# A hybrid decoder layer: the MLP's down projection by Strassen's seven products, token-major

## The chip, the cores and the metric

One core of a Trainium2 chip runs the whole layer in one launch. A core has five engines that work side by side and wait for each other through semaphores: TensorE (PE: matrix products into PSUM), VectorE (DVE), ScalarE (ACT), GpSimd (POOL) and SyncE (SP, which here only issues DMAs). Transfers run on 16 DMA engines that all queues share. The metric is the device time of one execution in microseconds, the median of the runs; lower is better.

## The reference

A pre-norm decoder layer on 512 tokens of width 1024, in float32. The first half (a gated DeltaNet, a convolution module and a cross-attention, merged through gates) is not touched. The second half is the conv-gated MLP, and a final norm:

```
h = rmsnorm(x, norm_ffn)
up = h @ w_up                                             # 1024 -> 2 x 2816
g_f = causal_dwconv(up[..., :2816], ffn_dw_w) + ffn_dw_b  # three taps along the tokens
x = x + (silu(g_f) * up[..., 2816:]) @ w_down             # 2816 -> 1024
return rmsnorm(x, norm_final)
```

## The kernel before

**Layout and precision.** Activations lie channel-major: a tile is 128 channels (partitions) by 512 tokens. Every large product is computed from high and low parts: `split` (L142) has ScalarE cast a tile to the matmul format (the high part) and VectorE subtract (the low part), and `proj` (L253) issues three matmuls for each slice of 128 of the contraction: high x high, high x low, low x high. The weight tile is the stationary operand, the activations move, 512 columns at a time.

**Weights.** They lie in DRAM as chunks of eight 128x128 tiles in order of use (512 KB). `fetch` (L223) loads chunk by chunk on SP's queue into four buffers `raw`, and splits each into `whi` and `wlo`, four buffers each. `wtile` (L244) asks for four chunks ahead. A tile is used by three matmuls, so a chunk lasts for 24.

**Order.** TensorE's and SP's instructions stand in the order in which the code issues them; for the other engines a scheduler chooses an order from its own estimates when the program is built. `run` (L153) interleaves a main generator with side generators, one step for each slice of `proj`. `paced` ties an instruction behind the last matmul issued, and `behind` (L104) ties VectorE's.

**The MLP.** `proj_o` (L1012) ends the first half and leaves the residual in eight tiles `x1`, and the scaled input's high and low parts `fh`, `fl`. `fnorm` (L1037) makes the norm's factors `rfb`. `ffn_up` (L1049) takes 22 slices j of the 2816 hidden channels; for each it makes the gate's product (tile `mm`) and the values' (tile `g`), 24 matmuls each; VectorE multiplies by `rfb` (L1059), ScalarE and VectorE do the taps (L1061, L1063), ScalarE the SiLU (L135), POOL multiplies by `rfb` again (L1067), VectorE by the values (L1069), and the result is split into `ah[j]`, `al[j]`, kept in SBUF.

`ffn_down` (L1084) takes output tiles of 128 channels: 22 slices, 66 matmuls into one PSUM bank; VectorE adds the result to `x1` (L1088), ScalarE squares it (L1090), VectorE sums the squares (L1094), ScalarE multiplies by the final norm's gain (L1096). That is so for seven tiles. The eighth is done in two halves of 256 tokens (`last_tile`, L1133), so that the norm and the stores of one half stand beside the other's matmuls. `final_norm` (L1109) sums the squares over channels with matmuls by a vector (L1114), takes the power -1/2 on POOL (L1116), spreads the factors over partitions with two transposes (L292), multiplies (L1127, L1125) and stores through ACT's and SP's queues (L1128).

Of the kernel before, what the change touches and what calls it, by code (L numbers as in the profile page):

```python
# [15 lines left out]
P = 128  # L16
# [6 lines left out]
WARM = 10  # L23
NSLOT = 74
# [13 lines left out]
        ("lnw", 4), ("lnb", 4), ("gateb", 24), ("nffn", KD), ("fdw", NJ * 3), ("fdb", NJ), ("nfin", KD),  # L38
# [16 lines left out]
def hybrid_kernel(ctx: ExitStack, tc: tile.TileContext, xT, memT, xtok, mtok, wall, vecs, cms, yT):  # L55
# [166 lines left out]

    def fetch(upto):  # L223
        while state[0] < min(upto, wall.shape[0]):
# [822 lines left out]
    ah, al = [], []  # L1047

    def ffn_up():  # L1049
        for j in range(NJ):  # L1050
            ps = MM()
            yield from proj(ps, fh, fl)
            pv = G()
            gv = proj(pv, fh, fl)
            for _ in range(8 if j == 0 else 1):
                next(gv)
                yield
            g = T(n="fg")
            V.tensor_tensor(g, ps, rfb, op=ALU.mult)  # L1059
# [10 lines left out]
            if j == NJ - 1:  # L1070
                free(*fh, *fl)
            a, b = T(dt=F32R, n="ah"), T(dt=F32R, n="al")
            split(c, a, b)
            free(c)
            ah.append(a)
            al.append(b)

    gf = fnorm()
    run(ffn_up(), (gf, 1))

    nsq = [None, None]
    HS = S // 2

    def ffn_down():  # L1084
        for o in range(KD - 1):
            ps = MM()
            yield from proj(ps, ah, al)
            V.tensor_tensor(x1[o], x1[o], ps, op=ALU.add)  # L1088
            s = T(n="sq")
            A.activation(s, x1[o], AF.Square)  # L1090
            if o == 0:
                nsq[0] = s
            else:
                V.tensor_tensor(nsq[0], nsq[0], s, op=ALU.add)  # L1094
                free(s)
            A.activation(x1[o], x1[o], AF.Copy, scale=vc("nfin", o))  # L1096

    rn, r0 = C((P, NT)), C((P, NT))

    def other_tiles():  # L1100

        yield from pause(6)
        ps = SM((P, NT))
        for t in range(NT):
            PE.matmul(ps[:, t:t + 1], nsq[0][:, sl(t)], mean, start=True, stop=True)
        V.tensor_scalar(r0, ps, EPS, None, op0=ALU.add)
        yield

    def final_norm(t0, t1):  # L1109

        c, n = slice(t0 * P, t1 * P), t1 - t0
        ps = SM((P, NT))
        for t in range(t0, t1):
            PE.matmul(ps[:, t:t + 1], nsq[1][:, sl(t)], mean, start=True, stop=True)  # L1114
        V.tensor_tensor(rn[:, t0:t1], r0[:, t0:t1], ps[:, t0:t1], op=ALU.add)
        G_.tensor_tensor(rn[:, t0:t1], rn[:, t0:t1], mhalf[:, :n], op=ALU.pow)  # L1116
        yield from pause(4)
        ps = G((P, n * P))
        bcast(ps, rn[:, t0:t1], n)
        w = 4 // n  # L1120
        for o in range(0, KD, w):
            y = T((P, w, n * P), n="y")
            for k in range(w):
                if o + k == KD - 1:
                    V.scalar_tensor_tensor(y[:, k], x1[o + k][:, c], vc("nfin", o + k), ps, op0=ALU.mult, op1=ALU.mult)  # L1125
                else:
                    V.tensor_tensor(y[:, k], x1[o + k][:, c], ps, op=ALU.mult)  # L1127
            (nc.sync if o // w % 2 else A).dma_start(yT[o:o + w, :, c].rearrange("o p c -> p o c"), y)  # L1128
        yield

    nsq[1] = T(n="sq")

    def last_tile(t0, t1):  # L1133
        c, n = slice(t0 * P, t1 * P), (t1 - t0) * P
        ps = MM()
        yield from proj(ps[:, :n], [t[:, c] for t in ah], [t[:, c] for t in al], at=pos[0])
        V.tensor_tensor(x1[KD - 1][:, c], x1[KD - 1][:, c], ps[:, :n], op=ALU.add)
        A.activation(nsq[1][:, c], x1[KD - 1][:, c], AF.Square)

    run(ffn_down())  # L1140
    run(last_tile(0, 2), (other_tiles(), 1))
    run(last_tile(2, 4), (chain(pause(4), final_norm(0, 2)), 1))
    drain(final_norm(2, 4))


# [11 lines left out]
def _layout(i):  # L1157
# [26 lines left out]
    parts.append(_tiles(g["w_down"][0]))  # L1184
# [7 lines left out]
    def taps(c):  # L1192
# [7 lines left out]
           "fdb": _cols(g["ffn_dw_b"][0]), "nfin": _cols(g["norm_final"]),  # L1200
# [17 lines left out]
    return {"xT": xT, "memT": memT, "xtok": g["x"][0].reshape(NT, P, D), "mtok": g["mem"][0].reshape(2, P, D), "wall": wall, "vecs": vecs, "cms": cms}  # L1218


_INS = ["xT", "memT", "xtok", "mtok", "wall", "vecs", "cms"]
# [19 lines left out]
```

## Time and profile before

| | us |
|---|---|
| median of 3 runs (lowest, highest) | 867.12 (866.92, 867.3) |
| the profiled execution | 866.9 |
| its span, first to last instruction | 865.1 |
| TensorE / VectorE / ScalarE / POOL busy | 853.5 / 541.8 / 356.5 / 92.7 |

Busy times are to be read against the span. A matmul's own duration is longer than its step: matmuls overlap in the array, so what one costs is the distance between two starts. The up projection goes from 493 to 733 us, the down projection from 733.4 to 855.5, and the end follows. An instruction that starts later than its predecessor's end has waited; the timeline shows in brackets for how long and for whom.

### The profile page before, as it was taken

The page shows a single profiled execution, that of the slowest core. Times are in us where ns is not written, and L with a number is a line of the kernel's source. Part 1 is how long each engine was busy: PE and PEld are TensorE (multiplying, and loading weights), DVE is VectorE, ACT ScalarE, POOL GpSimd, SP SyncE. Part 2 cuts the span into 40 slices and gives each one's busy share as a digit, 9 for nine tenths or more (in the row PEclk, how much of TensorE's full clock was granted, in tenths as well). Part 3 has the DMA queues.
Part 4 walks back from the last instruction along what each step waited for, and adds up shares of the span by engine and source line. Part 5 has one row for each costly group of instructions (what it writes and reads, how often), then busy time and mean ns, then how long its engine had stood idle before and what let it go on. Part 6 is the DMA issues. An engine that isn't in the chain of part 4 may idle for free.

```text
span 865.1 us, 11006 instructions
## 1 busy us (share of the span) xinstructions
PE 853.5 (99%) x4260; PEld 707.7 (82%) x4260; DVE 541.8 (63%) x852; ACT 356.5 (41%) x613; POOL 92.7 (11%) x103
## 2 busy tenths in 40 slices
PE   9999999999999999999999999999999999999996
PEld 7888788688877888888888888888888888888885
DVE  5885799869989999582385565555555555223223
ACT  7854676443333445353334443333333333223220
POOL 0100003400043010150000011111111111000000
PEclk9999999999999999999999999999999999999998
DMA  9753121352071222222334223332232322233202
GB/s 314 290 183 124 66 74 49 97 127 93 1 220 49 73 74 73 98 96 98 106 130 147 95 84 98 98 97 98 98 98 97 98 98 98 97 98 98 73 1 97
DMA packets 43556, 90.97 MB, mean 105 GB/s; under 512 B 15728, under 2 KB 20080, under 8 KB 43504
## 3 DMA queue, kind: packets, MB, share of 16 engines
q1 hardware_dynamic: 36144, 87.65, 30.5%
q10 hardware_dynamic: 7360, 2.62, 1.2%
q8 instruction: 33, 0.54, 0.3%
q14 instruction: 19, 0.16, 0.1%
HBM read 86.59 MB, written 3.67 MB: 104 GB/s over the span
## 4 chain that ended last, share of the span: by engine, by line
PE 93%; DVE 4%; issue 2%; ACT 1%; DMA 0%; POOL 0%; POOLq 0%; SPq 0%; DVEq 0%; ACTq 0%
PE mm L260 23%; PE mm L262 22%; PE mm L261 22%; PE g L262 5%; PE g L260 5%; PE g L261 5%; DVE wlo L146 1%; PE g L561 1%; PE g L559 1%; PE g L560 1%; DVE qkv L626 0%; DVE cc L597 0%; PE mm L397 0%; PE mm L396 0%; PE mm L398 0%
## 5 line engine op out<-in xcount | busy, mean ns | idle before, releaser
L145 ACT CAST whi<-raw 128x1024 fp32r<-128x1024 f32 (+1 forms) x150 | 154.4, 1029 | 300.5 <-PE mm L261 228.3
L146 DVE TENSOR_TENSOR wlo<-raw,whi 128x1024 fp32r<-128x1024 f32 (+1 forms) x150 | 181.1, 1207 | 112.9 <-ACT whi L145 112.0
L260 PE MATMUL mm<-hh,whi 128*128 128x512 f32 x352 | 143.4, 407 | 0.0
L262 PE MATMUL mm<-hh,wlo 128*128 128x512 f32 x352 | 137.6, 391 | 0.0
L261 PE MATMUL mm<-hl,whi 128*128 128x512 f32 x352 | 137.3, 390 | 0.0
L597 DVE SCALAR_TENSOR_TENSOR cc<-u,vec,cc 128x507 f32<-128x507 f32 (+19 forms) x120 | 87.1, 732 | 1.0
L262 PEld LDWEIGHTS mm<-hh,wlo 128*128 128x128 f32 x352 | 66.1, 188 | 14.5
L260 PEld LDWEIGHTS mm<-hh,whi 128*128 128x128 f32 x352 | 66.2, 188 | 13.3 <-issue 1.5
L261 PEld LDWEIGHTS mm<-hl,whi 128*128 128x128 f32 x352 | 66.3, 188 | 11.2
L260 PE MATMUL mm<-ah,whi 128*128 128x512 f32 (+1 forms) x198 | 72.6, 367 | 0.0
L261 PE MATMUL mm<-al,whi 128*128 128x512 f32 (+1 forms) x198 | 72.3, 365 | 0.0
L262 PE MATMUL mm<-ah,wlo 128*128 128x512 f32 (+1 forms) x198 | 72.3, 365 | 0.0
L260 PE MATMUL g<-fh,whi 128*128 128x512 f32 x176 | 68.6, 390 | 0.0
L260 PE MATMUL mm<-fh,whi 128*128 128x512 f32 x176 | 68.6, 390 | 0.0
L262 PE MATMUL g<-fh,wlo 128*128 128x512 f32 x176 | 68.5, 389 | 0.0
L262 PE MATMUL mm<-fh,wlo 128*128 128x512 f32 x176 | 68.5, 389 | 0.0
L261 PE MATMUL g<-fl,whi 128*128 128x512 f32 x176 | 68.5, 389 | 0.0
L261 PE MATMUL mm<-fl,whi 128*128 128x512 f32 x176 | 68.5, 389 | 0.0
L1067 POOL TENSOR_TENSOR fc<-fc,rfb 128x512 f32<-128x512 f32 x22 | 28.5, 1294 | 205.5 <-ACT fc L135 205.5
L1059 DVE TENSOR_TENSOR fg<-mm,rfb 128x512 f32<-128x512 f32 x22 | 15.2, 691 | 54.6 <-PE mm L262 54.6
L1069 DVE TENSOR_TENSOR fc<-fc,g 128x512 f32<-128x512 f32 x22 | 15.1, 688 | 46.9 <-POOL fc L1067 46.9
L261 PEld LDWEIGHTS mm<-al,whi 128*128 128x128 f32 x198 | 37.3, 189 | 6.1
(294 smaller groups left out, 1484.1 us busy)
## 6 DMA issues: line engine op xcount, KB each, us to landing
raw<-wall SPq DMA_DIRECT2D x142, 512.0 KB, 3.3
x<-xT SPq DMA_DIRECT2D x16, 256.0 KB, 4.2
raw<-wall SPq DMA_DIRECT2D x8, 256.0 KB, 5.8
tok<-xtok SPq DMA_DIRECT2D x8, 256.0 KB, 4.9
mraw<-memT SPq DMA_DIRECT2D x4, 256.0 KB, 6.2
tok<-mtok SPq DMA_DIRECT2D x4, 256.0 KB, 6.6
d_in<-at ACTq DMA_DIRECT2D x4, 256.0 KB, 3.0
yT<-y ACTq DMA_DIRECT2D x4, 256.0 KB, 2.4
```

The lines of the kernel that those rows point to most:

```text
L145: A.copy(hi, src)
L146: eng.tensor_tensor(lo, src, f(hi), op=ALU.subtract)
L260: PE.matmul(ps, hi, xh[k], start=(k == 0), stop=False)
L261: PE.matmul(ps, hi, xl[k], start=False, stop=False)
L262: last[0] = PE.matmul(ps, lo, xh[k], start=False, stop=(k == n - 1))
L559: PE.matmul(ps[h], hi, xh[k], start=(k == 0), stop=False)
L560: PE.matmul(ps[h], hi, xl[k], start=False, stop=False)
L561: PE.matmul(ps[h], lo, xh[k], start=False, stop=(k == KD - 1))
L597: paced(V.scalar_tensor_tensor(a[:, s:], u[c][:, :S - s], vc("dww", c * 31 + 30 - s), a[:, s:], op0=ALU.mult, op1=ALU.add))
L1059: V.tensor_tensor(g, ps, rfb, op=ALU.mult)
L1067: G_.tensor_tensor(c, c, rfb, op=ALU.mult)
L1069: V.tensor_tensor(c, c, pv, op=ALU.mult)
```

## The change

**Seven products.** The hidden channels are paired: the even slices of 128 are one half of the contraction, the odd ones the other. With 2 x 2 blocks (256 tokens; half the hidden channels; 512 output channels) the product is Strassen's, in Winograd's form, with seven block products in place of eight. The activations' slices are now the stationary operand (128 hidden channels by 128 tokens) and the weights move (512 output channels), so the result lies token-major: two PSUM banks of 128 tokens by 512 channels for each product. Each product is 11 slices x 2 token blocks x 3 matmuls.

**Sums of weights.** Four of the seven products need sums of weight blocks. `weight_sums` makes them in DRAM while the up projection runs: for each of 11 slices a plain DMA on SP's queue copies one summand (256 KB) to a DRAM tile, and three slots later a DMA on POOL's queue adds the second summand to it in place. A slot is 2 x SUMS = 6 steps, four sums take 4 x 14 slots. `blockfetch` then loads blocks, two at a time, in place of `fetch`.

**Sums of activations.** `ends` forms the differences of a pair of slices on VectorE, for the first EARLY = 8 pairs while the up projection runs; the other splits are issued from `prepare` during the down projection. POOL's product (L1067 before) goes to VectorE.

**Residual and norm.** `token_major` turns the residual by 32 transposes on TensorE, four at a time into the one bank `SM`, copied out by ScalarE. The products' results are added to it on VectorE (`upd`). The final norm's squares are now summed along the free dimension by ScalarE (`square`), and `store` scales and stores a block of 128 tokens. The last product does its last four slices block by block (STAG).

```
+        for dst, a, b in ((q1, w11, w12), (q2, q1, w22), (q3, w12, w22), (q4, q2, w21)):
+            for p in range(NP + 3):
+                if p < NP:
+                    paced(nc.sync.dma_start(dst[p], a[p]))
+                yield from pause(SUMS)
+                if p >= 3:
+                    paced(G_.dma_start(dst[p - 3], b[p - 3], accum_op=ALU.add))
+                yield from pause(SUMS)
...
+    blocks = q2 + w11 + q1 + q3 + w21 + w22 + q4
...
+    def blockfetch(upto):
+        while 2 * len(made) < min(upto, len(blocks)):
...
+            for i in range(n):
+                nc.sync.dma_start(raw[:, S * i:S * i + S], blocks[c + i])
...
+            split(raw[:, :S * n], hi[:, :S * n], lo[:, :S * n], eng=nc.vector)
...
+    def token_major():
+        for b in range(2):
+            for t in range(NT):
+                ps = SM((P, S))
+                for o in range(4):
+                    PE.transpose(ps[:, sl(o)], x1[4 * b + o][:, sl(t)], ident)
+                x1t[t][b] = T(n="x1t")
+                A.copy(x1t[t][b], ps)
+                yield from pause(3)
...
+    def ends(p):
+        a, b, e = a0[p], a1[p], T(n="e")
+        V.tensor_tensor(e[:, lo_], a[:, hi_], b[:, hi_], op=ALU.subtract)
+        V.tensor_tensor(e[:, hi_], a[:, lo_], e[:, lo_], op=ALU.subtract)
+        V.tensor_tensor(a[:, hi_], a[:, lo_], a[:, hi_], op=ALU.subtract)
...
+        V.tensor_tensor(e4[p // 2][:, HS * (p % 2):HS * (p % 2) + HS], b[:, lo_], e[:, hi_], op=ALU.subtract)
+        es[p] = pair(e)
...
-            G_.tensor_tensor(c, c, rfb, op=ALU.mult)
+            V.tensor_tensor(c, c, rfb, op=ALU.mult)
...
-            a, b = T(dt=F32R, n="ah"), T(dt=F32R, n="al")
-            split(c, a, b)
...
+    gf = chain(fnorm(), token_major())
+    gw = weight_sums()
+    run(ffn_up(), (gf, 1), (gw, 1))
...
+    def store(t, first):
+        n = 1 - first
+        square(t, n)
+        V.tensor_scalar(ssq[:, first, t:t + 1], ssq[:, first, t:t + 1], 1.0 / D, EPS, op0=ALU.mult, op1=ALU.add)
+        V.scalar_tensor_tensor(rn[:, t:t + 1], ssq[:, n, t:t + 1], 1.0 / D, ssq[:, first, t:t + 1],
+                               op0=ALU.mult, op1=ALU.add)
+        G_.tensor_tensor(rn[:, t:t + 1], rn[:, t:t + 1], mhalf[:, :1], op=ALU.pow)
+        V.tensor_tensor(x1t[t][first], x1t[t][first], nf[first], op=ALU.mult)
+        A.activation(x1t[t][first], x1t[t][first], AF.Copy, scale=rn[:, t:t + 1])
+        V.scalar_tensor_tensor(x1t[t][n], x1t[t][n], rn[:, t:t + 1], nf[n], op0=ALU.mult, op1=ALU.mult)
+        for b in range(2):
+            (nc.sync if b and first else A).dma_start(y[t][:, b * S:b * S + S], x1t[t][b])
...
+        prods = ((es, 1, ()),
+                 (a0, 0, ((0, 0, ADD),)),
+                 (es, 0, ((0, 1, ADD), (1, 1, ADD))),
+                 (a0, 1, ((1, 1, SUB), (1, 0, ADD))),
+                 (a1, 0, ((0, 0, ADD),)),
+                 (e4, None, ((0, 1, ADD),)),
+                 (a1, 1, ((1, 0, ADD),)))
...
+            for p, m in steps:
+                blockfetch((i * NP + p) // 2 * 2 + 8)
+                hi, lo = block(i * NP + p)
...
+                PE.matmul(ps[m], h[:, o:o + P], hi, start=(p == 0), stop=False)
+                PE.matmul(ps[m], h[:, o:o + P], lo, start=False, stop=False)
+                last[0] = PE.matmul(ps[m], l[:, o:o + P], hi, start=False, stop=(p == NP - 1))
...
+                    if i == 0:
+                        d6[m] = T(n="d6")
+                        A.copy(d6[m], ps[m])
+                    elif i == 1:
+                        V.tensor_tensor(d6[m], d6[m], ps[m], op=SUB)
+                        for tok, ch, op in ((0, 1, ADD), (1, 0, SUB), (1, 1, ADD)):
+                            upd(2 * tok + m, ch, d6[m], op)
```

`ffn_down`, `other_tiles`, `final_norm` and `last_tile` of before are gone. Up to the up projection's first matmul the program's instructions stand in the same order on every engine.

TensorE in the up projection, at the end of the second gate product, before (`fh`, `fl` are the input's parts, `whi`, `wlo` the weights'):

```order
L260 MATMUL mm_4583<-fh_4401,whi_4454 128x512
L261 MATMUL mm_4583<-fl_4402,whi_4454 128x512
L262 MATMUL mm_4583<-fh_4401,wlo_4455 128x512
L260 MATMUL mm_4583<-fh_4442,whi_4454 128x512
L261 MATMUL mm_4583<-fl_4443,whi_4454 128x512
L262 MATMUL mm_4583<-fh_4442,wlo_4455 128x512
L260 MATMUL mm_4583<-fh_4483,whi_4454 128x512
L261 MATMUL mm_4583<-fl_4484,whi_4454 128x512
L262 MATMUL mm_4583<-fh_4483,wlo_4455 128x512
L260 MATMUL g_4614<-fh_4197,whi_4495 128x512
```

and now; `sm` is the one bank for the transposes (L1106), `x` the residual tiles, `cm` the identity:

```order
L271 MATMUL mm_4640<-fh_4360,whi_4454 128x512
L272 MATMUL mm_4640<-fl_4361,whi_4454 128x512
L273 MATMUL mm_4640<-fh_4360,wlo_4455 128x512
L1106 MATMUL sm_4670<-cm,x_4163 128x128
L1106 MATMUL sm_4670<-cm,x_4203 128x128
L1106 MATMUL sm_4670<-cm,x_4244 128x128
L1106 MATMUL sm_4670<-cm,x_4285 128x128
L271 MATMUL mm_4640<-fh_4401,whi_4454 128x512
L272 MATMUL mm_4640<-fl_4402,whi_4454 128x512
L273 MATMUL mm_4640<-fh_4401,wlo_4455 128x512
```

A group of four transposes has come between the slices of one product; there are eight such groups.

VectorE in the down projection before, at the end of an output tile (`x` the residual, `mm` the product, `sq` the sums of squares):

```order
L1088 TENSOR_TENSOR x_4203<-x_4203,mm_6250 128x512
L1094 TENSOR_TENSOR sq_6247<-sq_6247,sq_6336 128x512
L146 TENSOR_TENSOR wlo_6356<-raw_6353,whi_6355 128x1024
L146 TENSOR_TENSOR wlo_6386<-raw_6383,whi_6385 128x1024
L146 TENSOR_TENSOR wlo_6416<-raw_6413,whi_6415 128x1024
L1088 TENSOR_TENSOR x_4244<-x_4244,mm_6340 128x512
L1094 TENSOR_TENSOR sq_6247<-sq_6247,sq_6426 128x512
L146 TENSOR_TENSOR wlo_6452<-raw_6449,whi_6451 128x1024
L146 TENSOR_TENSOR wlo_6482<-raw_6479,whi_6481 128x1024
L1088 TENSOR_TENSOR x_4285<-x_4285,mm_6430 128x512
```

and now, at the end of the second of the seven products (`d` holds the first product's result, `mm` the second's, `x1t` are the token-major residual tiles; `wlo` 6645 and 6668 are the low parts of the 15th and 16th pair of blocks):

```order
L1258 TENSOR_TENSOR d_6503<-d_6503,mm_6514 128x512
L1194 TENSOR_TENSOR x1t_4609<-x1t_4609,mm_6514 128x512
L1258 TENSOR_TENSOR d_6512<-d_6512,mm_6515 128x512
L1194 TENSOR_TENSOR x1t_4626<-x1t_4626,mm_6515 128x512
L1194 TENSOR_TENSOR x1t_4692<-x1t_4692,d_6503 128x512
L1194 TENSOR_TENSOR x1t_4658<-x1t_4658,d_6503 128x512
L1194 TENSOR_TENSOR x1t_4741<-x1t_4741,d_6503 128x512
L151 TENSOR_TENSOR wlo_6645<-raw_6641,whi_6644 128x1024
L1194 TENSOR_TENSOR x1t_4724<-x1t_4724,d_6512 128x512
L1194 TENSOR_TENSOR x1t_4675<-x1t_4675,d_6512 128x512
L1194 TENSOR_TENSOR x1t_4776<-x1t_4776,d_6512 128x512
L151 TENSOR_TENSOR wlo_6668<-raw_6664,whi_6667 128x1024
```

In place of one or two additions between three weight subtractions, seven operations stand ahead of one, and three more ahead of the next.

## Rows read from the trace of the kernel before

**Rows 1.** The page, part 1: busy time, share of the span, instructions.
```profile
PE 853.5 (99%) x4260; PEld 707.7 (82%) x4260; DVE 541.8 (63%) x852; ACT 356.5 (41%) x613; POOL 92.7 (11%) x103
```

**Rows 2.** Windows; the first row names the columns.
```profile
core 0: us, PE busy (x) PEld busy (x) DVE busy (x) ACT busy (x) POOL busy (x), PEclk, DMA share, GB/s
...
39.30:49.60 10.30, 10.30 (x47) 8.51 (x47) 10.30 (x16) 5.81 (x8) 0.00 (x0) 1.00 0.55 178
506.00:733.00 227.00, 227.00 (x1003) 187.95 (x1002) 121.51 (x147) 86.59 (x106) 27.71 (x22) 1.00 0.30 98
733.40:838.10 104.70, 104.70 (x464) 86.69 (x463) 31.92 (x32) 28.23 (x32) 0.36 (x1) 1.00 0.23 76
```

**Rows 3.** Timeline of TensorE, first and last matmuls of the down projection (start, duration).
```profile
733.37 0.39 PE L260 MATMUL mm<-ah,whi 128*128 128x512 f32 x1
...
838.09 0.28 PE L260 MATMUL mm<-ah,whi 128*128 128x256 f32 x1
...
855.33 0.28 PE L262 MATMUL mm<-ah,wlo 128*128 128x256 f32 x1
```

**Rows 4.** Lines by form, TensorE, 733.3 to 865 us (count | busy, mean ns | idle).
```profile
L260 PE MATMUL mm<-ah,whi 128*128 128x512 f32 x154 | 59.9, 389 | 0.0
...
L260 PE MATMUL mm<-ah,whi 128*128 128x256 f32 x44 | 12.7, 288 | 0.0
```

**Rows 5.** Timeline of the other engines behind the last matmul.
```profile
855.65 0.42 DVE L1137 TENSOR_TENSOR x<-x,mm 128x256 f32<-128x256 f32 x1 [1.87 <-PE mm L262]
...
857.21 0.16 DVE L1115 TENSOR_TENSOR c<-c,sm 128x2 f32<-128x2 f32 x1 [1.15 <-PE sm L1114]
857.45 0.70 POOL L1116 TENSOR_TENSOR c<-c,mhalf 128x2 f32<-128x2 f32 x1 [7.29 <-DVE c L1115]
...
861.25 0.47 DVE L1125 SCALAR_TENSOR_TENSOR y<-x,vec,g 128x256 f32<-128x256 f32 x1
```

**Rows 6.** Timeline of TensorE, the memory's value projection, first and last of 48 matmuls.
```profile
39.34 0.39 PE L396 MATMUL mm<-whi,mh 128*128 128x512 f32 x1
...
49.99 0.39 PE L398 MATMUL mm<-whi,ml 128*128 128x512 f32 x1
```

**Rows 7.** Timeline of TensorE, a group of four transposes between matmuls.
```profile
109.66 0.39 PE L262 MATMUL mm<-hh,wlo 128*128 128x512 f32 x1
109.89 0.60 PE L531 MATMUL g<-cm,e 128*128 128x128 f32 x4
110.24 0.47 PE L260 MATMUL mm<-hh,whi 128*128 128x512 f32 x1
110.56 0.39 PE L261 MATMUL mm<-hl,whi 128*128 128x512 f32 x1
```

**Rows 8.** Line L337, a 512-wide square with its read-out on ScalarE (min/median/max ns).
```profile
L337 ACT ACTIVATE sq<-tok x12: 615/632/636, 17.4 to 31.1; 128x512 f32<-128x512 f32 x12
L337 ACT ACTIVATION_READ_ACCUMULATOR sq<-tok x12: 183/186/188, 17.9 to 31.6; 128x1 f32 x12
```

**Rows 9.** The page, part 6: DMA issues, count, KB each, us to landing.
```profile
raw<-wall SPq DMA_DIRECT2D x142, 512.0 KB, 3.3
```

**Rows 10.** Lines by form, all engines, 490 to 865 us.
```profile
L146 DVE TENSOR_TENSOR wlo<-raw,whi 128x1024 fp32r<-128x1024 f32 x63 | 77.2, 1225 | 61.9 <-ACT whi L145 61.9
...
L145 ACT CAST whi<-raw 128x1024 fp32r<-128x1024 f32 x63 | 66.4, 1055 | 155.2 <-PE mm L261 127.7 <-PE g L261 20.5 <-issue 7.0
...
L1063 DVE SCALAR_TENSOR_TENSOR fc<-fg,vec,fc 128x511 f32<-128x511 f32 x22 | 16.4, 745 | 0.9 <-ACT fc L1061 0.9
...
L1088 DVE TENSOR_TENSOR x<-x,mm 128x512 f32<-128x512 f32 x7 | 4.8, 686 | 13.3 <-PE mm L262 13.3
```

**Rows 11.** DMA queue of ACT, 173 to 181 us (packets, MB, share of 16 engines).
```profile
q10 hardware_dynamic: 1451, 0.73, 31.7%
```

**Rows 12.** DMA queue of ACT, 183 to 190 us.
```profile
q10 hardware_dynamic: 4162, 0.53, 47.8%
```

More of the change, by code (lines that the diff above doesn't have):

```diff
@@ L221, in hybrid_kernel @@
     pos = [0]
+    NW = wall.shape[0]
+    beyond = [None]
     def fetch(upto):
-        while state[0] < min(upto, wall.shape[0]):
+        if upto > NW and beyond[0]:
+            beyond[0](2 * (upto - NW))
+        while state[0] < min(upto, NW):
             c = state[0]
@@ L1044, in fnorm, with weight_sums @@
         yield
[L1047 removed]
+    NP = NJ // 2
+    HS = S // 2
+    w11, w12, w21, w22 = [[wdn[p, i, :, S * b:S * b + S] for p in range(NP)] for i in range(2) for b in range(2)]
+    q1, q2, q3, q4 = [[dp.tile([P, S], F32, name=nm("q")) for _ in range(NP)] for _ in range(4)]
+    def weight_sums():
+        for dst, a, b in ((q1, w11, w12), (q2, q1, w22), (q3, w12, w22), (q4, q2, w21)):
[6 more added lines that the diff above has]
+                yield from pause(SUMS)
@@ new lines, in hybrid_kernel @@
+    beyond[0] = blockfetch
+    x1t = [[None, None] for _ in range(NT)]
+    def token_major():
[7 more added lines that the diff above has]
+                yield from pause(3)
+            free(*x1[4 * b:4 * b + 4])
+    a0, a1, es, e4 = [None] * NP, [None] * NP, [None] * NP, [None] * ((NP + 1) // 2)
@@ L1084, in ffn_down @@
-    def ffn_down():
[L1085 to L1143, printed above, removed]
+            if j % 2:
+                a1[j // 2] = c
+                if j // 2 < EARLY:
+                    ends(j // 2)
+            else:
+                a0[j // 2] = c
@@ new lines, in hybrid_kernel, with block, prepare @@
+    gf = chain(fnorm(), token_major())
+    gw = weight_sums()
+    run(ffn_up(), (gf, 1), (gw, 1))
+    drain(gw)
+    free(*fh, *fl, rfb)
+    nf = []
+    def block(i):
+        hi, lo = made[i // 2]
+        c = slice(S * (i % 2), S * (i % 2) + S)
+        return hi[:, c], lo[:, c]
+    def prepare():
+        for p in range(EARLY, NP):
+            ends(p)
+            yield
+        for p in range(NP):
+            a0[p] = pair(a0[p])
+            yield
+        yield from pause(EARLY)
+        for p in range(NP):
+            a1[p] = pair(a1[p])
+            yield
+            yield
+        for p in range(0, NP, 2):
+            e4[p // 2] = pair(e4[p // 2], min(2, NP - p) * HS)
+            yield
+            yield
@@ new lines, in hybrid_kernel @@
+    ADD, SUB = ALU.add, ALU.subtract
+    d6 = [None, None]
+    def ffn_down():
+        prods = ((es, 1, ()),
[5 more added lines that the diff above has]
+                 (a1, 1, ((1, 0, ADD),)))
+        gp = prepare()
+        for i, (tiles, half, outs) in enumerate(prods):
+            lastp = i == len(prods) - 1
+            ps = [MM() if i % 2 else G() for _ in range(2)]
+            steps = [(p, m) for p in range(NP) for m in range(2)]
+            if lastp:
+                e = NP - STAG
+                steps = steps[:2 * e] + [(p, m) for m in range(2) for p in range(e, NP)]
+            for p, m in steps:
+                blockfetch((i * NP + p) // 2 * 2 + 8)
+                hi, lo = block(i * NP + p)
+                h, l = tiles[p] if tiles is not e4 else tiles[p // 2]
+                o = HS * (half if half is not None else p % 2) + m * P
+                PE.matmul(ps[m], h[:, o:o + P], hi, start=(p == 0), stop=False)
+                PE.matmul(ps[m], h[:, o:o + P], lo, start=False, stop=False)
+                last[0] = PE.matmul(ps[m], l[:, o:o + P], hi, start=False, stop=(p == NP - 1))
+                if m:
+                    behind[0] = last[0] if i * NP + p > NP else None
+                    next(gp, None)
+                    behind[0] = None
+                    if tiles is es and half == 0 or tiles is a0 and half == 1 or tiles is a1 and half == 1:
+                        free(h, l)
+                    elif tiles is e4 and (p % 2 or p == NP - 1):
+                        free(h, l)
+                if p == NP - 1:
+                    if i == 0:
[5 more added lines that the diff above has]
+                            upd(2 * tok + m, ch, d6[m], op)
+                        free(d6[m])
+                    for tok, ch, op in outs:
+                        upd(2 * tok + m, ch, ps[m], op)
+                    if i == 3:
+                        nf.append(T(n="nf"))
+                        nc.sync.dma_start(nf[m], nfin[:, m * S:m * S + S])
+                        square(2 + m, 1)
+                    elif i == 4:
+                        square(m, 0)
+                    elif i == 5:
+                        store(m, 0)
+                    elif i == 6:
+                        store(2 + m, 1)
+                yield
```

53 lines of the change are left out of this document (35 added, 18 removed).

## The prediction

> **What bounds the kernel now.** I read the busy times first: TensorE is busy for 853.5 of 865.1 us [rows 1], so only work taken off it, or off what follows its last instruction, can count. Then the windows: in the MLP's up projection (506 to 733 us) and its down projection (733.4 to 838.1 us) TensorE has no idle time, the granted clock is 1.00 (2.4 GHz), VectorE is busy for 121.5 of 227 and for 31.9 of 104.7 us, and the DMA engines for 0.30 and 0.23 [rows 2]. Then the timeline: a matmul of 512 columns follows the one before after 0.2267 us: from 733.37 to 838.09 are 462 of them, 104.72 us; the last output tile goes in two token halves, whose 132 matmuls of 256 columns step by 0.12 us, with small matmuls of the norm between, until 855.33 + 0.12 = 855.45 [rows 3, 4]. From there to the end of the span are 9.65 us: one chain through every engine [rows 5]. The profiled execution took 866.9 us (span 865.1, and 1.8 around it); the median of the runs is 867.12, 0.2 above.
>
> **The products.** Before, the down projection is 8 output tiles x 22 slices of the contraction x 3 (high and low parts) = 528 matmuls of 512 columns, the last 66 as 132 halves. After, 7 products x 11 x 2 token blocks x 3 = 462 of 512 columns: exactly the part that now ends at 838.09. The 17.36 us from 838.09 to 855.45 go, small matmuls of the norm included: **-17.4 us**. Operands change sides (activations stationary, weights moving). The memory's value projection runs in that form already: its 48 matmuls go from 39.34 to 49.99, 47 steps of 0.2266 us [rows 6], so the price of one stays.
>
> **The residual.** 32 transposes of 128x128 enter TensorE's row in the up projection, in 8 groups of 4. A group of 4 at 109.89 shows the price: the second matmul behind it starts at 110.56, where it would have started at 109.66 + 2 x 0.2267 = 110.11 without the group: 0.44 us [rows 7]. 8 x 0.44 = **+3.5 us**. All groups share one PSUM bank, which ScalarE must copy out (some 0.6 us, as a 512-wide square on it [rows 8]) before the next group starts; groups stand three steps (2.0 us) apart, and a copy can stand behind a cast, a SiLU or its table load. From 0 to 0.5 us for each group; I take 0.5 in all, since most have 1.4 us to spare.
>
> **Weights.** A block of 128x512 feeds 6 matmuls, 1.36 us, where a 512 KB chunk fed 24, 5.44 us: twice the rate, 193 GB/s, at a DMA share of about 0.30 x 193/98 = 0.59. The memory's value projection asks for the same rate: 0.55 of the DMA engines, VectorE busy for all 10.3 us, and no idle time on TensorE [rows 2]. A pair of blocks (12 matmuls, 2.72 us) has four buffers, so 10.9 us pass between two uses of one; landing 3.3 [rows 9], cast 1.05, subtraction 1.23 [rows 10] are 5.6. Cost nothing; if it failed, the third rival.
>
> **VectorE.** In the up projection a pair of slices (21.8 us) gives it 4 weight subtractions, 2 x (product, two taps, the product that POOL had, product with the values), and 4 half-wide subtractions with a split: 4.9 + 7.1 + 2.4 = 14.4 us, 66%: hidden. In the down projection it has, counted in the order, 35 weight subtractions at 1.225, 24 updates and 31 other full-width operations at 0.69, and small ones, about 84 of 104.7 us; products 2 and 3 (products and pairs are counted from 0) alone hold 11 weight subtractions, 16 updates and 12 splits, 13.5 + 11.0 + 8.3 = 32.8 us in 30.2 [rows 10]. What was made ahead must cover it. I step through the order from the end of product 1 (29.7 us after the projection's start; pair n is wanted at 2.72n + 0.23): seven updates end at 34.5, pair 14 is split at 35.7 (wanted 38.3), three more updates, pair 15 at 39.0 (41.0), pair 16 at 41.6 (43.7), 17 at 44.2 (46.5), 18 at 46.1 (49.2), then the four updates of product 2 at 49.6, and pair 19 at 50.8, wanted at 51.9. The least spare time is 1.1 us. That each is just in time bounds the wait at 0 and, with nothing made ahead, 2.6; I take 0.5. Waits in all **+1.0 us**.
>
> **Sums in DRAM.** 44 plain copies on SP's queue and 44 adding transfers on POOL's, 256 KB each, one of each every 6 steps (4.08 us) of the up projection. POOL has nothing else left there; its wait for a copy holds back no one until the norm at the end. SP's copies of the second and fourth sum wait for an addition, and weight loads stand behind them, but that addition was issued some 45 us before. So the DMA engines decide. The up projection's 0.30 for 98 GB/s makes 0.80 us of all 16 engines for 256 KB; into DRAM from the chip it is 0.317 x 8 us for 0.73 MB, 0.91 per 256 KB; the dearest transfer, in small packets, 0.478 x 7 us for 0.53 MB, 1.65 [rows 2, 11, 12]. No row shows DRAM to DRAM, or an addition. A group of 14 slots is 57.1 us; weights take 17.1, 11 copies at 0.9 take 9.9, so 30.1 us are left for 11 additions: 2.7 us each are hidden. An addition reads two operands and writes one: between 0.8 (one pass) and 5.0 (three passes at the dearest price); I take 0.8 + 0.9 = 1.7, nearest the rows of full-size packets: **0 us**. The Trainium skill (Collectives: The Full Stack, "The bandwidth ceiling: the fold count and why AG ≠ RS ≠ AR") says that an add within a transfer is slowed by its second source read and not by the adding, half the rate of a copy; no run here shows it. By that rule an addition would be 1.6 us, and the sum the same.
>
> **The end.** Before, from 855.45: 0.20 to the update at 855.65, and so on to 861.72, then 3.38 to the end [rows 5]. After, the last token block's chain is 0.20, update 0.69, square with its read-out 0.63 + 0.19, a small operation 0.16, POOL's power 0.70, the last product 0.75 [rows 5, 8, 10], and some 0.3 for hand-overs: 3.6. The block before it ends its matmuls 2.72 us sooner and its 3.4 us on VectorE stand in front: +0.7. Then 3.4 and, since two 256 KB stores leave together, up to 0.5. Together 8.2 against 9.65: **-1.5 us**.
>
> Sum: 866.9 - 17.4 + 3.5 + 1.0 - 1.5 = 852.5; on the runs' median **852.7 us**, 1.7% faster. By itself this case holds 850.5 (no waits, and an end without the 1.2 us of the last two terms) to 855.5 (2.6 us on VectorE and 0.7 more at the transposes).
>
> **Rivals.**
> - VectorE becomes the bound of products 1 to 3, the pairs' low parts coming late. For it: 32.8 us of work in 30.2, eight updates in a row at one product's end, 1.1 us of spare time. Against it: VectorE was full in the memory's value projection and TensorE did not wait [rows 2]. With nothing ahead 2.6 us, and as much again if the splits of the first product, of which VectorE puts several ahead of the last up slice's own work, delay pair 3 and after: 855.5 to 858.5. Chance 0.14.
> - The additions fill the DMA engines (the case on the other side). Above 2.7 us each, the rest is owed by the weight loads: 44 x (c - 2.7) less the gain of 14.4, slower from c = 3.0. At c = 4: 57 - 14 = 43 us slower, 910; at 5.0, 954. For it: nothing in the trace shows such a transfer, and the bound of 5.0 lies beyond. Against it: full-size packets, not small ones. Chance 0.08, of which 0.01 for a rule beside it. The Trainium skill (SBUF — State Buffer, "SBUF: two separate sides") says that transfers issued by POOL get no descriptors while VectorE runs a copy that takes both its ports to SBUF; in these stages VectorE's program has operations of two sources instead, and no run here shows it.
> - Weights at twice the rate come late: pairs of blocks each as long as a landing, 3.3 instead of 2.72 us, over 38.5 pairs +22 us: 875. Against it: four loads can be in flight. Chance 0.03.
> - Nothing gained, because waits of 14 us in all arise in many places: 867, chance 0.02.
>
> **How the numbers follow.** Forecast 0.73, and the four rivals. About 0.2% (1.7 us) is what a measurement of this kernel can tell from no change. Faster: 0.73 + 0.14 = 0.87; within 0.2%: the last rival and a mild form of the DMA cases, 0.02 + 0.01 = 0.03; slower: the rest of the DMA cases, 0.10. The range goes from 850.5 to 860, over the first rival, and leaves out the DMA cases.
>
> **What would show it.** Right: TensorE without idle time from 493 us on at clock 1.00; 462 matmuls 0.2267 apart in the down projection, with it starting 3.5 to 4 us later than 733.4 and ending near 842; about 8 us after that. Copies and additions end before the up projection does, with a DMA share of 0.6 to 0.9. Wrong: TensorE waiting for low parts behind the updates (first rival), SP's weight loads issued late and TensorE waiting for casts in the up projection with the DMA share at its ceiling (second), raw blocks landing late in the down projection (third). A transposing group that costs 1 us or more would also break the sum.

## The result, and the profile after

The changed kernel takes 852.23 us (median of 4 runs, 852.21 to 852.27) where the kernel before takes 867.02 (4 runs on the same chip, 866.77 to 867.3): a ratio of 0.9829, 95% interval 0.9812 to 0.9846. The prediction said 852.7, within 850.5 to 860. The profiled execution took 852.23 with a span of 850.3 us, 14.8 less than the 865.1 of before.

TensorE is still what bounds the kernel. The page's busy times, against [rows 1]:

```profile
PE 839.1 (99%) x4140; PEld 693.1 (82%) x4140; DVE 607.5 (71%) x958; ACT 385.1 (45%) x661; POOL 100.2 (12%) x127
```

14.4 us are gone from TensorE, in 120 matmuls fewer; VectorE has 66 us more. The windows of the up projection and of the down projection, to be read against the last two of [rows 2]:

```profile
core 0: us, PE busy (x) PEld busy (x) DVE busy (x) ACT busy (x) POOL busy (x), PEclk, DMA share, GB/s
506.00:733.00 227.00, 227.00 (x1015) 187.91 (x1014) 142.47 (x195) 82.22 (x101) 30.97 (x38) 1.00 0.73 189
738.30:842.00 103.70, 103.70 (x459) 85.88 (x458) 78.75 (x105) 56.56 (x78) 1.10 (x2) 1.00 0.55 175
```

TensorE has no idle time in either, at a granted clock of 1.00 (2.4 GHz). What the change added shows elsewhere: the DMA share rose from 0.30 to 0.73 and from 0.23 to 0.55, VectorE's load in the down projection from 31.9 us to 78.8.

TensorE's first and last matmul of the down projection, the places of [rows 3]:

```profile
738.22 0.39 PE L1242 MATMUL g<-whi,ah 128*128 128x512 f32 x1
...
842.71 0.39 PE L1244 MATMUL g<-whi,al 128*128 128x512 f32 x1
```

The last of 462 starts 104.49 us behind the first, 461 steps of 0.2267 without a gap, and 0.23 later, at 842.94, TensorE is done; before, that was at 855.45.

One of the eight groups of transposes, as [rows 7]:

```profile
502.94 0.40 PE L273 MATMUL g<-fh,wlo 128*128 128x512 f32 x1
503.18 0.60 PE L1106 MATMUL sm<-cm,x 128*128 128x128 f32 x4
503.53 0.48 PE L271 MATMUL g<-fh,whi 128*128 128x512 f32 x1
503.85 0.39 PE L272 MATMUL g<-fl,whi 128*128 128x512 f32 x1
```

The second matmul behind the group starts 0.91 us after the one ahead of it, where two steps are 0.45: 0.46 for the group, and no wait for the PSUM bank.

The chain behind the last matmul, VectorE, ScalarE and POOL, against [rows 5]:

```profile
843.38 0.68 DVE L1194 TENSOR_TENSOR x1t<-x1t,g 128x512 f32<-128x512 f32 x1
844.09 0.63 ACT L1200 ACTIVATE sq<-x1t 128x512 f32<-128x512 f32 x1 [0.66 <-DVE x1t L1194]
844.62 0.19 ACT L1200 ACTIVATION_READ_ACCUMULATOR sq<-x1t 128x1 f32 x1
844.84 0.16 DVE L1208 SCALAR_TENSOR_TENSOR c<-c 128x1 f32<-128x1 f32 x1 [0.79 <-ACT sq L1200]
845.08 0.55 POOL L1210 TENSOR_TENSOR c<-c,mhalf 128x1 f32<-128x1 f32 x1 [2.41 <-DVE c L1208]
...
845.66 0.75 DVE L1213 SCALAR_TENSOR_TENSOR x1t<-x1t,c,nf 128x512 f32<-128x512 f32 x1 [0.66 <-POOL c L1210]
```

From 842.94 to the end of the span are 7.36 us (before: 9.65): 0.44 to the update, 3.03 through the engines to 846.41, 3.89 for the last two stores and what the program does behind them.

**Where the 14.8 us come from.** Four differences between the two traces make up the whole of it:

| stretch | before | after | difference |
|---|---|---|---|
| start to the first transposes of the up projection's norm | 497.14 | 498.15 | +1.0 |
| from there to the first matmul of the down projection | 236.23 | 240.07 | +3.8 |
| to TensorE's last matmul's end | 122.08 | 104.72 | -17.36 |
| to the end of the span | 9.65 | 7.36 | -2.3 |

The first line was not in the prediction: the instructions are the same there, though not the places of their data (see `wide_constants`).

### The profile page after: what moved, and what is told of

Its sections match the earlier page's. It is cut to its first block, busy times and chain, and to the rows that moved or that the text cites. A ratio compares the mean times of both kernels' runs of the same rounds, so it can differ in the third digit from the quotient of the medians.

```text
span 850.3 us, 11186 instructions
## 1 busy us (share of the span) xinstructions
PE 839.1 (99%) x4140; PEld 693.1 (82%) x4140; DVE 607.5 (71%) x958; ACT 385.1 (45%) x661; POOL 100.2 (12%) x127
## 4 chain that ended last, share of the span: by engine, by line
PE 91%; DVE 5%; issue 1%; DMA 1%; ACT 1%; SPq 0%; POOL 0%; POOLq 0%; DVEq 0%; ACTq 0%
PE mm L271 18%; PE mm L272 17%; PE mm L273 17%; PE g L271 5%; PE g L272 5%; PE g L273 5%; PE g L1244 2%; PE g L1242 2%; PE g L1243 2%; PE mm L1244 2%; PE mm L1242 2%; PE mm L1243 2%; DVE wlo L151 1%; DVE cc L608 1%; PE g L572 1%
## 5 line engine op out<-in xcount | busy, mean ns | idle before, releaser
L150 ACT CAST whi<-raw 128x1024 fp32r<-128x1024 f32 (+1 forms) x167 | 171.9, 1029 | 282.3 <-PE mm L272 171.9
L151 DVE TENSOR_TENSOR wlo<-raw,whi 128x1024 fp32r<-128x1024 f32 (+1 forms) x167 | 201.0, 1204 | 75.6 <-ACT whi L150 74.2
L273 PEld LDWEIGHTS mm<-hh,wlo 128*128 128x128 f32 x352 | 66.1, 188 | 14.4
L1077 POOL DMA_DIRECT2D q<-wdn x44 | 36.2, 991 | 161.1 <-DMA q<-q 98.4
L273 PEld LDWEIGHTS g<-fh,wlo 128*128 128x128 f32 x176 | 33.1, 188 | 7.0
L273 PEld LDWEIGHTS mm<-fh,wlo 128*128 128x128 f32 x176 | 33.0, 187 | 7.0
L271 PEld LDWEIGHTS mm<-fh,whi 128*128 128x128 f32 x176 | 33.1, 188 | 6.8
L272 PEld LDWEIGHTS g<-fl,whi 128*128 128x128 f32 x176 | 33.1, 188 | 6.6
L271 PEld LDWEIGHTS g<-fh,whi 128*128 128x128 f32 x176 | 33.0, 187 | 6.7
```

The lines of the kernel that those rows point to most:

```text
L150: A.copy(hi, src)
L151: eng.tensor_tensor(lo, src, f(hi), op=ALU.subtract)
L271: PE.matmul(ps, hi, xh[k], start=(k == 0), stop=False)
L272: PE.matmul(ps, hi, xl[k], start=False, stop=False)
L273: last[0] = PE.matmul(ps, lo, xh[k], start=False, stop=(k == n - 1))
L1077: paced(G_.dma_start(dst[p - 3], b[p - 3], accum_op=ALU.add))
```

## The experiments

The theory is the prediction's: the path is TensorE's row of matmuls, so the gain is the saved product and the end, less the transposes, and what was added on VectorE, POOL and the DMA engines lies beside it. The rivals are that one of these added works is paid for in part, or is near its limit.

### The saved product alone: eight_products

The four blocks are multiplied in the usual way, in the same token-major form, with the same transposes and end; no sums are made, neither in DRAM nor on VectorE. The main piece of the edit:

```
-        prods = ((es, 1, ()),
...
-                 (a1, 1, ((1, 0, ADD),)))
+        prods = ((a0, 0, ((0, 0, ADD),)), (a0, 0, ((0, 1, ADD),)), (a1, 0, ((0, 0, ADD),)), (a1, 0, ((0, 1, ADD),)),
+                 (a0, 1, ((1, 0, ADD),)), (a0, 1, ((1, 1, ADD),)), (a1, 1, ((1, 0, ADD),)), (a1, 1, ((1, 1, ADD),)))
-    blocks = q2 + w11 + q1 + q3 + w21 + w22 + q4
+    blocks = w11 + w12 + w21 + w22 + w11 + w12 + w21 + w22
```

> The down projection keeps its token-major form, its transposed residual and its end, but multiplies the four blocks in the usual way: eight products, no sums in DRAM and none on VectorE. Theory (the whole gain is the product that is saved): 66 more matmuls at 0.2267 us are 15.0 us, 867.2, within 0.7: the time of the kernel before, so that the token-major form by itself is worth nothing (its transposes cost what its shorter end gives back). Rival (Strassen's extra work on VectorE, POOL and the DMA engines costs something beside): less than 13 us slower than the changed kernel, below 865.2.

867.51 us (11 runs; ratio to the kernel before 1.0002, 0.9993 to 1.0011). TensorE's row in the down projection goes from 738.54 to 858.22, 119.68 us, 14.96 more than with seven products, and the end takes 7.48. The theory holds: without the saved product nothing of the gain is left, and Strassen's sums cost nothing that this comparison can tell.

### The transposes: no_turn

```
-                ps = SM((P, S))
-                for o in range(4):
-                    PE.transpose(ps[:, sl(o)], x1[4 * b + o][:, sl(t)], ident)
-                A.copy(x1t[t][b], ps)
+                A.copy(x1t[t][b], x1[4 * b + t])
```

> The 32 transposes of the residual are left out; ScalarE copies the untransposed tile in the same place, so the output is another. Theory (8 groups of 4 cost 0.44 us each on TensorE and nothing else): 3.5 us faster, 848.7, within 0.4. Rival (the groups also make matmuls wait for ScalarE's copies or delay the casts): faster by 4.5 us or more. Other rival (part of them is hidden): faster by 2.5 us or less.

848.38 us (848.0 to 850.46, 4 runs): 3.85 faster between medians. TensorE's row tells it more exactly. The spread of the norm's factors and the first matmul of the down projection in this kernel:

```profile
501.63 0.60 PE L303 MATMUL g<-cm,c 128*128 128x128 f32 x4
...
733.98 0.39 PE L1239 MATMUL g<-whi,ah 128*128 128x512 f32 x1
```

They are 232.35 us apart, in the kernel before too (501.02 to 733.37), and 236.18 in the changed kernel (502.04 to 738.22). The eight groups cost 3.83 us, 0.48 each, and nothing beside.

### The sums in DRAM: none, twice, three times, and all at once

`no_sums` leaves the transfers out; `twice_sums` (first piece below; the copies likewise) and `thrice_sums` issue each of them two and three times, the extra ones into DRAM tiles of their own; `sums_at_once` (second piece) issues the same 44 pairs at three times the pace:

```
                     paced(G_.dma_start(dst[p - 3], b[p - 3], accum_op=ALU.add))
+                    paced(G_.dma_start(d2[p - 3], w22[p - 3], accum_op=ALU.add))
```

```
-SUMS = 3
+SUMS = 1
```

> The 44 copies and 44 adding transfers are left out; products 0, 2, 3 and 6 read plain blocks of the weight instead of sums, so the output is another. Theory (the transfers lie wholly beside TensorE's work): the time stays at 852.2, within 0.4 us, while the DMA engines' share in the up projection falls from 0.73 to about 0.30. Rival (they hold up weight loads a little at a time, and TensorE with them): faster by 1 us or more, to 851.2 or below.

851.67 us (851.26 to 852.16), 0.56 below the changed kernel, just outside the 0.4 expected and short of the rival's 1. The DMA share in the up projection is 0.29, and TensorE is busy for all of 506 to 733 us in both. From the first transposes to the end of TensorE's last matmul both traces have 344.79 us (498.56 to 843.35 here, 498.15 to 842.94 in the changed kernel), so the 0.56 does not lie there: TensorE lost nothing to the sums.

> Every copy and every adding transfer is issued twice, the second into a DRAM tile that nobody reads. In the changed kernel's trace the 44 additions took 75.9 us of all 16 DMA engines, 1.72 each, and the copies about 0.68 each. Theory (what limits is the time of the DMA engines): the share in the up projection would be 0.30 + 2 x 0.42 = 1.15 of 227 us, so 34 us do not fit; part of it is made up behind the up projection, and the kernel takes 875 to 890. Rival 1 (the sums only lag behind, the weight loads keep their share, and the sums are wanted late enough): below 856. Rival 2 (POOL, which takes 1 us to issue one and waits for copies, is the limit): the DMA share stays below 0.9, and the time is above 860 all the same.

853.25 us (853.23 to 853.56): rival 1, and the theory is wrong here. The DMA queues' part of the page of the changed kernel (packets, MB, share of 16 engines over the span) and its list of issues (count, KB each, median us to landing):

```profile
q0 software_dynamic: 6336, 11.54, 8.9%
...
q<-wdn POOLq DMA_DIRECT2D x44, 256.0 KB, 6.2
```

8.9% of 850.3 us are 75.7, 1.72 us of all 16 engines for one addition. With twice the sums:

```profile
q0 software_dynamic: 12672, 23.07, 14.9%
...
506.00:733.00 227.00, 227.00 (x1016) 187.91 (x1014) 141.66 (x194) 81.99 (x101) 66.83 (x82) 1.00 1.05 283
```

That is 126.9 us for 88: with twice as many in the queue each took 1.44 of the engines' time. The share is 1.05, landings took 10.8 us instead of 6.2, and TensorE did not wait. The 1.0 us over the changed kernel lies behind TensorE's last matmul, which starts at 842.66; the chain behind it is the same, and the packets of the last stores end at 848.7 in both traces, but the span ends at 851.5 instead of 850.3. Why was not tested.

> Every copy and every adding transfer is issued three times, the second and third into DRAM tiles that nobody reads. With twice as many the up projection's DMA share was 1.05 and TensorE did not wait; the share grew by 0.32 for 44 pairs of transfers. Theory (the DMA engines' time is the limit, and twice was just below it): 1.05 + 0.32 = 1.37 of 227 us, 84 us too much, of which some 20 lie before and behind in idle stretches: 900 to 930, with TensorE waiting for weight casts in the up projection. Rival (the sums give way to the weight loads and only the first products wait for their sums): 853 to 870, with the wait at the start of the down projection. Other rival (POOL's issue is the limit): POOL busy without a pause, and the DMA share under 0.95.

932.54 us (931.11 to 933.85; ratio to the kernel before 1.0752, 1.0734 to 1.077): the theory, 2.5 us beyond its upper end. Three windows, and TensorE's longest waits from 493 us on (total, times, longest):

```profile
554.00:578.00 24.00, 24.00 (x108) 19.87 (x107) 15.18 (x21) 6.12 (x8) 8.94 (x11) 1.00 1.09 285
578.00:602.00 24.00, 22.60 (x97) 17.76 (x96) 11.75 (x17) 6.56 (x8) 7.31 (x9) 1.00 1.09 272
602.00:626.00 24.00, 16.90 (x60) 12.76 (x58) 9.07 (x14) 4.16 (x5) 8.12 (x10) 0.79 1.08 275
```

```profile
PE mm L271 <- ACT whi L150: 21.2, 8, 8.1
PE g L271 <- ACT whi L150: 19.9, 9, 7.1
```

The DMA engines stand at 1.08 to 1.09 of what the view calls full, weight casts come late, and where TensorE waits most the granted clock falls too, to 0.79 in the third window. But from 506 to 578 us, under the same load, TensorE did not wait.

> The same 44 copies and 44 additions, but one of each every two steps (1.36 us) instead of every six: all within the first 80 us of the up projection. Theory (what counts is what the DMA engines are asked for at the time): 0.30 + 3 x 0.36 = 1.4 of them in that stretch, the load of the run with three times the sums, which cost 80 us over 240: some 80/3 = 27 us, 875 to 885. Rival (only the total counts; the transfers queue up and the weight loads keep their share): 852 to 854.

852.37 us (851.9 to 852.45): the rival. The load was there, and TensorE did not feel it:

```profile
506.00:560.00 54.00, 54.00 (x253) 44.70 (x252) 30.75 (x43) 20.42 (x27) 19.47 (x24) 1.00 1.09 271
560.00:600.00 40.00, 40.00 (x178) 33.15 (x177) 25.37 (x35) 14.64 (x18) 9.90 (x13) 1.00 1.08 309
```

Weights landed after 10.9 us in the median from 506 to 602 us, against 16.5 in the run with three times the sums. What my expectation left out is that loads are asked for four chunks of 5.44 us ahead, 21.8 us, of which a landing of 3.3 and a cast and a subtraction of 1.05 and 1.23 [rows 9, 10] use 5.6. This lead has to be used up before TensorE waits: three times the sums began to hurt between 578 and 602 us, and at once the last addition is issued at 584. That the lead is the cause fits both runs, but no run changed the lead alone. Nor did one take the copies off SP's queue, in which the weight loads stand behind them: how much of the lateness in `thrice_sums` is full engines and how much that queue is not separated.

### VectorE's reserve: ten_updates and twentyfour_updates

VectorE repeats updates at the end of product 1, where the prediction saw it closest to its limit: four times for 24 additions, as below, and `2 - tok * ch` times for ten.

```
                             upd(2 * tok + m, ch, d6[m], op)
+                            for _ in range(4):
+                                upd(2 * tok + m, ch, d6[m], op)
```

> Ten more VectorE additions of 128x512 stand behind the updates of product 1 (blocks of the residual are added several times over, so the output is another). In the changed kernel's trace VectorE starts such additions 0.60 us apart, the high-low subtractions 1.14 to 1.21 apart, and the least time between a low part's end and its first matmul is 3.05 us (pair 15). Theory (VectorE has 3 us in hand there and gains on TensorE with every later pair, and splits that are wanted later can stand back): 10 x 0.60 = 6.0 us cost 0 to 1.5 us: 852.2 to 853.7. Rival (the prediction's account, 1.1 us in hand at 0.69 each): 6.9 - 1.1 = 5.8 us, 858.

852.6 us (851.84 to 852.92), no wait of TensorE: the theory. Why the prediction's reserve of 1.1 us was too small is seen in the changed kernel's VectorE timeline at that place:

```profile
772.04 1.22 DVE L151 TENSOR_TENSOR wlo<-raw,whi 128x1024 fp32r<-128x1024 f32 x1
773.18 1.89 DVE L1194 TENSOR_TENSOR x1t<-x1t,d 128x512 f32<-128x512 f32 x3
774.99 1.21 DVE L151 TENSOR_TENSOR wlo<-raw,whi 128x1024 fp32r<-128x1024 f32 x1
776.12 1.28 DVE L118 TENSOR_TENSOR al<-fc,ah 128x512 fp32r<-128x512 f32 x2
```

Three additions take 1.81 us from start to the next operation's start, 0.60 each, not 0.69, and a subtraction of 1.22 gives way after 1.14: instructions in a row overlap. The low part of pair 15 ends at 776.20 and is wanted at 738.22 + 15 x 2.72 + 0.23 = 779.25, a reserve of 3.05 us, the least of all pairs. With ten more additions the least is 0.79 (pair 17).

> As the run with ten, with 24 more additions: 14.4 us. Theory (VectorE has 3 us in hand, some 4.5 idle us up to 813 and some more behind; beyond that TensorE waits for low parts or for PSUM): 3 to 8 us slower than the changed kernel, 855 to 860, with TensorE's waits in products 2 to 4. Rival (VectorE is never a bound in the down projection, since work wanted later gives way): within 1 us of 852.2. Rival (VectorE was full there, every added us counts): 14 us slower, 866.

862.45 us (861.44 to 862.61), 10.2 slower: more than the theory's 3 to 8, less than the 14 of the second rival. TensorE waits 0.2 us for the low part of a weight, and then once for that of an activation:

```profile
PE g L1244 <- DVE al L118: 6.9, 1, 6.9
PE g L1243 <- DVE wlo L151: 0.2, 1, 0.2
```

The order in which VectorE's work is done is made anew for each kernel, and here it put that split behind the added work, so the reserve is bracketed, not measured: 6.0 us are free, 14.4 are not. The clock fell too, in the 15 us that hold the wait, and most of all behind it (second row):

```profile
798.00:813.00 15.00, 7.84 (x23) 5.62 (x22) 15.00 (x23) 5.18 (x9) 0.00 (x0) 0.77 0.43 153
...
807.60:813.00 5.40, 5.40 (x13) 4.24 (x14) 5.40 (x10) 3.49 (x7) 0.00 (x0) 0.52 0.28 97
```

The matmul behind the wait starts at 807.60 and the next at 808.19, 0.59 us later instead of 0.23; the ones after it step by 0.43 until 812.46. A granted clock of 0.52 is nearly the lower of the two levels, 1.2 GHz.

### The 1 us ahead of the MLP: before_again and wide_constants

> The kernel before, once more with a profile. The up projection's first transposes came at 497.14 us in the first profile of it, and at 498.15, 498.13, 498.56, 498.47 and 497.74 in five profiles of kernels whose program is the same until there. Theory (this is a scatter between executions, from transfers that a chain of small matmuls waits for around 256 us): somewhere from 497.1 to 498.6. Rival (the changed kernel's layout of its constants makes it late): again 497.1, within 0.15.

866.92 us, and the first transposes at 497.15: the rival's number, so this is not mere scatter. The two us in which the traces part, in the kernel before once more, and then in the changed kernel:

```profile
258.00:260.00 2.00, 2.00 (x38) 1.19 (x37) 1.89 (x5) 1.92 (x5) 1.92 (x5) 1.00 0.05 14
```

```profile
258.00:260.00 2.00, 1.07 (x28) 0.55 (x31) 1.87 (x5) 1.55 (x3) 1.92 (x5) 1.00 0.55 201
```

TensorE waits there 0.9 us for a small VectorE copy in the chain that inverts blocks, and the DMA share shows that transfers which were over by then in the kernel before still ran in the changed kernel.

```
-        ("lnw", 4), ("lnb", 4), ("gateb", 24), ("nffn", KD), ("fdw", NJ * 3), ("fdb", NJ),
+        ("lnw", 4), ("lnb", 4), ("gateb", 24), ("nffn", KD), ("fdw", NJ * 3), ("fdb", NJ), ("pad", KD),
```

> The changed kernel with eight unused columns where the constants of the final norm stood before, so that the constants lie as in the kernel before. Two profiles of the kernel before have the up projection's first transposes at 497.14 and 497.15 us, eight of kernels with the changed layout at 497.74 to 498.67, though the order of the instructions is the same until there. Theory (the layout of the constants on chip makes 1 us): 497.15, within 0.15. Rival (it is something else, such as where the tensors lie in DRAM): 497.7 to 498.7.

851.89 us, the first transposes at 497.86: the rival's number. But that number adds up two things, which the traces part. The start of the program does not take the same time in every profile: the first matmul of the memory's value projection stands at 39.34 and 39.24 us in the two of the kernel before, at 40.08 here, and between 39.20 and 40.36 in the ten with the changed layout. From there to the first transposes are 457.80 and 457.91 us in the kernel before, 457.78 here, and 458.40 to 458.95 in the ten. In the two us of the wait, with the eight columns, TensorE has no gap, although the DMA engines are busy here too:

```profile
258.00:260.00 2.00, 2.00 (x70) 1.27 (x68) 1.87 (x5) 1.23 (x4) 1.92 (x5) 1.00 0.43 168
```

The traces part earlier, at a store of 128 KB. VectorE's wait for it, in the kernel before, in the changed kernel, and with the eight columns:

```profile
243.98 0.55 DVE L594 TENSOR_SCALAR cc<-u,vec 128x512 f32<-128x512 f32 x1 [0.85 <-DMA d_out<-tit]
...
244.22 0.55 DVE L605 TENSOR_SCALAR cc<-u,vec 128x512 f32<-128x512 f32 x1 [1.28 <-DMA d_out<-tit]
...
244.59 0.55 DVE L605 TENSOR_SCALAR cc<-u,vec 128x512 f32<-128x512 f32 x1 [0.76 <-DMA d_out<-tit]
```

The wait is 0.76 to 0.85 us in the three profiles with the old layout and 1.27 to 1.33 in the ten with the new one (1.29 in `no_sums`, whose start is as late as here, at 40.16), and TensorE's wait around 258 us (0.3 to 0.9 us) is in all of these ten and in none of the three. So the layout of the constants is the cause, as the theory had it, at 0.5 to 1.2 us, and what made `wide_constants` miss its number is the 0.7 us by which its start was late, within the spread of the ten. Why the place of the constants makes this store slower, and whether it is their place on the chip or in DRAM, stays open.

### A shorter end: early_end

```
-STAG = 4
+STAG = 7
...
+        for c, q in ((lo_, nc.sync), (hi_, A)):
+            V.scalar_tensor_tensor(x1t[t][n][:, c], x1t[t][n][:, c], rn[:, t:t + 1], nf[n][:, c],
+                                   op0=ALU.mult, op1=ALU.mult)
+            q.dma_start(y[t][:, n * S:n * S + S][:, c], x1t[t][n][:, c])
+        nc.sync.dma_start(y[t][:, first * S:first * S + S], x1t[t][first])
```

> Of the last product the last seven steps, not four, are done first for one token block and then for the other, and the last block's output leaves in three stores, its first 128 KB as soon as that half is scaled. In the changed kernel the last block's first update waited 0.24 us for VectorE, which was at the block before it, and 3.9 us pass from VectorE's last operation to the end of the span. Theory (both lie on the path): 0.24 us and 0.2 to 0.5 us for the stores, so 851.5 to 851.8. Rival (the stores' end is a fixed time after the last issue): 852.0.

851.35 us (851.02 to 852.82, 5 runs; ratio to the kernel before 0.9817, 0.9803 to 0.983, which overlaps the changed kernel's). Medians and intervals don't tell it from the changed kernel. In the trace the last matmul ends at 843.86:

```profile
844.05 0.69 DVE L1194 TENSOR_TENSOR x1t<-x1t,g 128x512 f32<-128x512 f32 x1 [1.72 <-PE g L1251]
...
846.35 0.88 DVE L1219 SCALAR_TENSOR_TENSOR x1t<-x1t,c,nf 128x256 f32<-128x256 f32 x2 [0.66 <-POOL c L1210]
```

The update follows after 0.19 instead of 0.44 us, and the span ends at 850.8, 3.57 us behind VectorE's last operation instead of 3.89; the two half operations took 0.13 longer than the one. In all 6.94 instead of 7.36 us, 0.42, just under the theory's 0.44 to 0.74. Only the 0.25 at the update are clear: the stretch from the last matmul's end to the end of the span takes 7.05 to 7.48 us in eight profiles that end with the same chain (and 8.61 in `twice_sums`), so what the split store brings is not shown.

## Why the prediction was right

Its main term was right and carried the result; two smaller ones were too cautious by 0.7 and 0.8 us, and one was missing, so the sum came within 0.5 us partly because these cancel: -17.36 + 3.83 - 2.29 + 1.0 = -14.8, where it had -17.4 + 4.5 - 1.5 = -14.4.

- **The products:** -17.4 predicted, -17.36 in the trace, and 14.96 for one product in `eight_products`. That turned operands keep the price of one matmul, read from the memory's value projection [rows 6], holds.
- **The residual:** 3.5 predicted from [rows 7], 3.83 measured; the 0.5 for the shared PSUM bank did not come. ScalarE's copies took 0.57 to 0.59 us, and the groups stand 2.5 us apart.
- **VectorE:** 0.5 predicted, 0 measured. The step that was mis-sized is the walk through VectorE's order, which added up durations [rows 10], where starts in a row are 0.60 and 1.14 us apart: products 2 and 3 hold the 32.8 us that it counted, and VectorE is busy in them (768.15 to 798.07) for 27.77 of 29.92 us. The first rival (0.14) named the right place, but it begins only after more than 6 us of added work.
- **Weights** at twice the rate were in time: loads of blocks landed after 2.8 us (sums) and 3.3 (plain) in the median.
- **Sums in DRAM:** 1.7 us of 16 engines for an addition were predicted, 1.72 measured, and the time is hidden. That the two agree is in part luck: the 1.7 was put together from other transfers, and a plain copy cost 0.64, not 0.9 (queue q1, which carries all plain transfers of that stretch, takes 39.8% of the engines from 490 to 735 us, and 28.3% in `no_sums`: 28 us for 44 copies). The Trainium skill (Collectives: The Full Stack, "The bandwidth ceiling: the fold count and why AG ≠ RS ≠ AR") says half the rate of a copy, 1.6 by the prediction's estimate; the runs decide otherwise: 1.72, some 2.7 times the 0.64 of a copy in the same stretch, and 1.44 to 1.46 where the engines were full (`thrice_sums`: 20.7% of 930.7 us for 132). The bound of 2.7 us each was too low, since twice the sums are hidden too. The second rival's mechanism is real, 80 us in `thrice_sums`, but its condition was not met; its rule that all above the bound is owed at once left out the lead of the loads, which fits the runs but was not tested by itself.
- **The end:** -1.5 predicted, -2.29 measured: the update waited 0.24 us for VectorE, not 0.7, POOL's power took 0.55, not 0.70, the read-out begins 0.53 us after its square, not 0.63, and the hand-overs took 0.17, not 0.3. The 3.9 us from VectorE's last operation to the end were met.
- **Missed:** +1.0 us ahead of the MLP, which the prediction took as unchanged because its instructions are. The constants lie otherwise, and with them a store around 240 us lands later and TensorE waits around 258: +1.15 us from the memory's value projection on, and -0.14 ahead of it.

## What to carry to other kernels

Where one engine's row has no gaps, count what leaves that row and what follows its last instruction: the rest of a large change, here 88 transfers and 47 us of VectorE work in the down projection, was worth nothing either way. But ask of each hidden work how much more would fit, since it is no slope but a step: twice the transfers cost at most 1 us, three times as many cost 80. Price a run of short VectorE instructions by the distance of their starts, not by the sum of their durations. And a stage whose instructions are unchanged can still change: eight columns of constants fewer cost 0.5 to 1.2 us in a stage that does not use them. Where a number adds up several stretches, compare the stretches before the number is taken as a verdict.

## What the runs showed of the hardware

- An adding transfer of 256 KB between DRAM tiles took 1.72 us of all 16 DMA engines at a share of 0.73, and 1.44 at 1.05; it landed after 6.2 us, and after 15.7 in the fullest run.
- The DMA share stood at 1.08 to 1.09 for some 80 us without TensorE losing anything, in a kernel that asks for its loads some 20 us ahead.
- A TensorE wait cost more than itself: the granted clock was 0.77 to 0.79 over windows of 15 and 24 us with waits in them, 0.52 over the 5.4 us behind the longest wait of the run with 24 more updates, and there 7.1 us of waiting went with 10.2 us of time.
- Eight columns of constants more or fewer changed VectorE's wait for one store of 128 KB from 0.76 to 0.85 us to 1.27 to 1.33, in 3 and 10 profiles.
